# A fused two-layer MLP in bf16: another way in for the first block's input, and another order for its second product

## The chip, the cores and the metric

One core of one Trainium2 chip runs the whole program. The metric is the device time of one execution in microseconds, as a median over runs.

## The reference

```python
x  = randn(8, 1024, 1024)      # float32
w1 = randn(1024, 4096)
w2 = randn(4096, 1024)
h = x @ w1
h = 0.5 * h * (1 + tanh(sqrt(2 / pi) * (h + 0.044715 * h ** 3)))
return (h @ w2).astype(float32)
```

There are 8192 tokens. Each goes through 1024 to 4096 columns, GELU, and 4096 to 1024 columns. In 128x512 matmuls (a 128x128 block of weights against 512 columns) that is 4096 for the first product and 4096 for the second.

## The kernel before

Tokens are taken in 16 blocks of 512. Both weights are cast to bf16 by the load and stay in SBUF, the on-chip memory. A block's x has to be turned so that the hidden dimension lies on the partitions. The kernel writes a bf16 copy of it to DRAM (`phase0`), and reads that back through the transposing DMA (`xbar`). The head of the program queues block 0's x, then w1, then block 1's x copies, then w2:

```python
def load_w1(j):                      # eight loads, 1 MB each as stored
    nc.gpsimd.dma_start(out=w1_sb[:, :, j*512:(j+1)*512], in_=w1r[:, :, j*512:(j+1)*512])
def load_w2(j):                      # eight loads of four 128-row chunks
    nc.gpsimd.dma_start(out=w2_sb[:, j*4:(j+1)*4, :], in_=w2r[:, j*4:(j+1)*4, :])
# ... cut
for hc in range(HC):
    phase0(0, hcs=[hc])              # strided copy of x into DRAM, as bf16
    xbar(0, hcs=[hc])                # transposing DMA into xT
# ... cut
for j in range(NW1):
    load_w1(j)
if NB > 1:
    phase0(1)
for j in range(NW2):
    load_w2(j)
for b in range(NB):
    # ... cut: xbar(b + 1), phase0(b + 2)
    g = mm1_gelu(b)                  # 32 chunks of 8 matmuls, GELU per two chunks
    mm2_store(b, g)
```

The second product goes slice after slice: 128 tokens run through all 32 chunks of w2 before the next 128 tokens begin.

```python
def mm2_store(b, g):
    for s in range(TSUB):                          # four slices of 128 tokens
        po = psum_o.tile([P, OC, NFREE], F32)
        for ic in range(IC):                       # 32 chunks of w2
            for oc in range(OC):
                nc.tensor.matmul(po[:, oc, :], lhsT=g[:, ic, s*P:(s+1)*P],
                                 rhs=w2_sb[:, ic, oc*NFREE:(oc+1)*NFREE],
                                 start=(ic == 0), stop=(ic == IC - 1))
        o_sb = opool.tile([P, OC, NFREE], F32)
        nc.vector.tensor_copy(out=o_sb, in_=po)
        # ... cut: store o_sb
```

## Time and profile before

| | before |
|---|---|
| time, median of 13 runs | 1821.73 us (1819.48 to 1823.04) |
| TensorE busy, of the profiled span | 1768.4 of 1820.8 us |
| first block-0 matmul | 20.2 us |
| block 1's first matmul | 158.2 us |
| last matmul, about | 1816 us |

(The prediction was made on the first four of these runs, with a median of 1822.65 us.)

The first part of the profile's page gives busy time by engine. PE is TensorE's matmuls, PEld its weight loads, which run beside them; DVE is VectorE, ACT is ScalarE, POOL is GpSimd; x is the number of instructions recorded:

```profile
PE 1768.4 (97%) x8029; PEld 803.1 (44%) x8192; DVE 78.4 (4%) x64; ACT 263.2 (14%) x257; POOL 92.0 (5%) x148
```

No other engine is busy for more than 15% of the span. The steady rate comes from a stretch table: from 300 to 400 us it counts 464 weight loads, one for each matmul, so about 0.2155 us each. The 256 matmuls of block 1's first product (158.20 to 213.45 us) give 0.2158 us, the figure used below. 8192 of them take about 1768 us. Some 50 us are not matmuls at full rate, and TensorE's timeline for the first 220 us shows where they are. Its columns are start, duration, engine, line, operation, tiles, count, and in brackets the idle time before and what ended it:

```profile
20.17 1.89 PE L117 MATMUL ph<-xT,w_sb 128*128 128x512 bf16 x4 [20.17 <-DMA w_sb<-in_w_dram]
24.51 0.58 PE L117 MATMUL ph<-xT,w_sb 128*128 128x512 bf16 x1 [2.46 <-DMA xT<-xb]
27.97 0.59 PE L117 MATMUL ph<-xT,w_sb 128*128 128x512 bf16 x1 [2.87 <-DMA xT<-xb]
31.47 0.58 PE L117 MATMUL ph<-xT,w_sb 128*128 128x512 bf16 x1 [2.92 <-DMA xT<-xb]
34.90 56.20 PE L117 MATMUL ph<-xT,w_sb 128*128 128x512 bf16 x244 [2.84 <-DMA xT<-xb]
90.93 8.80 PE L137 MATMUL po<-w_sb,g 128*128 128x512 bf16 x40
101.37 1.89 PE L137 MATMUL po<-w_sb,g 128*128 128x512 bf16 x7 [1.64 <-DMA w_sb<-in_w_dram]
106.99 2.78 PE L137 MATMUL po<-w_sb,g 128*128 128x512 bf16 x8 [3.74 <-DMA w_sb<-in_w_dram]
112.10 46.26 PE L137 MATMUL po<-w_sb,g 128*128 128x512 bf16 x196 [2.33 <-DMA w_sb<-in_w_dram]
158.20 55.42 PE L117 MATMUL ph<-xT,w_sb 128*128 128x512 bf16 x251
```

The waits of the same engine, summed by what they waited for:

```profile
PE ph L117 <- DMA w_sb<-in_w_dram: 20.2, 1, 20.2
PE ph L117 <- DMA xT<-xb: 11.1, 4, 2.9
PE po L137 <- DMA w_sb<-in_w_dram: 7.7, 3, 3.7
```

Read them together. TensorE does nothing for 20.2 us. It then gets x one piece at a time until 34.9 us, when only seven matmuls are done. The first product then runs without a break, if slowly at first. Slice 0 of the second product starts at 90.9 us and catches up with the w2 loads, which it waits for three times, until 112.1 us. From 158.2 us on nothing is lost any more.

The third loss is a matter of rate. In this stretch table (columns: stretch, length, then for each engine busy time and number of instructions, granted TensorE clock, share of the DMA engines, GB/s) only 10 and 16 matmuls are recorded in two 4 us stretches that elsewhere hold 19 to 21:

```profile
112.00:116.00 4.00, 3.90 (x10) 1.43 (x10) 0.29 (x1) 0.00 (x0) 3.10 (x6) 0.50 1.81 178
116.00:120.00 4.00, 4.00 (x16) 1.57 (x14) 0.93 (x1) 0.00 (x0) 2.47 (x5) 0.74 1.98 171
120.00:124.00 4.00, 3.95 (x19) 1.86 (x19) 0.00 (x0) 0.00 (x0) 1.80 (x3) 1.00 1.81 167
```

The granted clock (the share of TensorE's full clock that the profile records) is 0.50 and 0.74 there: after the waits the matmuls start again at half speed. They do so at 34.9 us as well, where the weight loads stand 0.43 us apart until 39.55 us. (The clock column says 1.00 in that first stretch, so the spacing is the safer sign.)

### The profile page before, as it was taken

How to read it: one execution, taken by the hardware profiler on the slowest of the kernel's cores; microseconds unless marked ns; L12 is line 12 of the kernel's file. 1: busy time of each engine (PE TensorE's matmuls, PEld its weight loads, DVE VectorE, ACT ScalarE, POOL GpSimd, SP SyncE). 2: the span in 40 equal slices, each digit the busy share in tenths (PEclk: the TensorE clock that was granted, in tenths of full speed). 3: DMA queues.
4: the chain of work that ended last, by engine and by line, in shares of the span. 5: the costliest groups of instructions: out<-in, count | busy, mean ns of one | idle time of the engine just before them, and what ended most of it. 6: DMA issues, size and time to landing. Idle time of an engine off the chain costs nothing.

```text
span 1820.8 us, 17187 instructions
## 1 busy us (share of the span) xinstructions
PE 1768.4 (97%) x8029; PEld 803.1 (44%) x8192; DVE 78.4 (4%) x64; ACT 263.2 (14%) x257; POOL 92.0 (5%) x148
## 2 busy tenths in 40 slices
PE   3989999999999999999999999999999999999998
PEld 1434444444444444444444444444444444444444
DVE  0000010000000000000000000000000000000000
ACT  0201202011030210202012020110202102020120
POOL 3237300000000000000000000000000000000000
PEclk9989999999999999999999999999999999999999
DMA  9999910101001010010101101010010100100001
GB/s 174 198 195 194 117 47 1 47 24 35 35 1 58 12 35 35 15 44 12 47 24 23 47 1 46 24 35 35 1 58 12 35 35 15 44 12 24 24 0 47
DMA packets 159047, 85.02 MB, mean 47 GB/s; under 512 B 138496, under 2 KB 146688, under 8 KB 158976
## 3 DMA queue, kind: packets, MB, share of 16 engines
q0 software_dynamic: 80128, 33.56, 14.8%
q1 hardware_dynamic: 78848, 50.35, 9.4%
q8 instruction: 64, 1.05, 0.3%
q14 instruction: 7, 0.06, 0.0%
HBM read 67.11 MB, written 50.33 MB: 65 GB/s over the span
## 4 chain that ended last, share of the span: by engine, by line
PE 93%; DMA 5%; issue 1%; POOL 1%; DVE 0%; POOLq 0%
PE po L137 48%; PE ph L117 45%; DMA w_sb<-in_w_dram 5%; DMA xb<-in_x_dram 0%; POOL w_sb L73 0%; POOL xb L92 0%; DVE o_sb L145 0%; POOLq L185 0%
## 5 line engine op out<-in xcount | busy, mean ns | idle before, releaser
L117 PE MATMUL ph<-xT,w_sb 128*128 128x512 bf16 x4016 | 886.9, 380 | 35.5 <-DMA w_sb<-in_w_dram 20.2
L137 PE MATMUL po<-w_sb,g 128*128 128x512 bf16 x4013 | 886.4, 380 | 12.0 <-DMA w_sb<-in_w_dram 7.7
L117 PEld LDWEIGHTS <-w_sb 128*128 128x128 bf16 x4096 | 401.4, 98 | 518.0 <-DMA w_sb<-in_w_dram 20.2
L137 PEld LDWEIGHTS <-g 128*128 128x128 bf16 x4096 | 401.7, 98 | 494.4 <-issue 13.4
L124 ACT ACTIVATE g<-ph 128x1024 bf16<-128x1024 f32 x256 | 261.9, 1023 | 1497.9 <-PE ph L117 1478.4
L145 DVE COPY o_sb<-po 128x1024 f32<-128x1024 f32 x64 | 78.4, 1224 | 1738.9 <-PE po L137 1701.1
L92 POOL DMA_DIRECT2D xb<-in_x_dram x128 | 78.8, 617 | 109.3 <-DMA w_sb<-in_w_dram 82.2
L64 POOL DMA_DIRECT2D w_sb<-in_w_dram x8 | 7.0, 898 | 1.3 <-DMA xb<-in_x_dram 1.3
L73 POOL DMA_DIRECT2D w_sb<-in_w_dram x8 | 6.0, 781 | 0.2 <-issue 0.2
L124 ACT ACT_TABLE_LOAD x1 | 1.3, 1283 | 0.7 <-PEq L185 0.7
L185 POOL MEMSET const-float32-0.0<- 128x1 f32 x1 | 0.1, 98 | 0.2 <-issue 0.2
L185 POOL MEMSET const-bfloat16-1.0<- 128x1 bf16 x1 | 0.1, 101 | 0.0
L185 POOL MEMSET const-float32-1.0<- 128x1 f32 x1 | 0.1, 98 | 0.0
L185 POOL MEMSET const-uint8-127<- 128x1 uint8 x1 | 0.1, 98 | 0.0
## 6 DMA issues: line engine op xcount, KB each, us to landing
out_dram<-o_sb SPq DMA_DIRECT2D x64, 512.0 KB, 3.8
xb<-in_x_dram POOLq DMA_DIRECT2D x128, 128.0 KB, 5.6
w_sb<-in_w_dram POOLq DMA_DIRECT2D x16, 1024.0 KB, 30.5
xT<-xb SPq DMA_TRANSPOSE x128, 2.6
```

The source lines that it names most:

```text
L64: nc.gpsimd.dma_start(out=w1_sb[:, :, j * W1_COL:(j + 1) * W1_COL], in_=w1r[:, :, j * W1_COL:(j + 1) * W1_COL],)
L73: nc.gpsimd.dma_start(out=w2_sb[:, j * W2_ROWG:(j + 1) * W2_ROWG, :], in_=w2r[:, j * W2_ROWG:(j + 1) * W2_ROWG, :],)
L92: nc.gpsimd.dma_start(out=xb[hc], in_=xr[hc])
L117: nc.tensor.matmul(ph[:, k, :], lhsT=w1_sb[:, hc, ic * P:(ic + 1) * P], rhs=xT[:, hc, :], start=(hc == 0), stop=(hc == HC - 1),)
L124: nc.scalar.activation(out=g[:, ig * IPB:(ig + 1) * IPB, :], in_=ph, func=GELU,)
L137: nc.tensor.matmul(po[:, oc, :], lhsT=g[:, ic, s * P:(s + 1) * P], rhs=w2_sb[:, ic, oc * NFREE:(oc + 1) * NFREE], start=(ic == 0), stop=(i ...
L145: nc.vector.tensor_copy(out=o_sb, in_=po)
L185: nc = _bacc.Bacc("TRN2", target_bir_lowering=False, num_devices=1)
```

## The change

It wants to start TensorE earlier and to stop it from waiting for w2. It has four parts:

- **x of block 0** comes by four plain loads into SBUF, is transposed by TensorE against an identity, and is copied by VectorE from PSUM, the memory that the matmuls' results go to here.
- **w1** comes in smaller pieces: the first 512 columns in eight (one for each hidden chunk), the others in four each. **w2** comes in 32 pieces.
- **Block 0's second product** goes through w2 chunk by chunk, with all four slices accumulating at once.
- **PSUM**: that needs four accumulators, so the two pools of two buffers become one pool of four.

```diff
-    psum_h = ... bufs=2          psum_o = ... bufs=2
+    pspool = ... bufs=4
-    def load_w1(j):
-        nc.gpsimd.dma_start(out=w1_sb[:, :, c0:c1], in_=w1r[:, :, c0:c1])
+    def load_w1(j, split):
+        for h0 in range(0, HC, HC // split):
+            h1 = h0 + HC // split
+            nc.gpsimd.dma_start(out=w1_sb[:, h0:h1, c0:c1], in_=w1r[:, h0:h1, c0:c1])
 # ... cut: load_w2 by single chunks
+        if ic_major:
+            pos = [pspool.tile([P, OC, NFREE], F32, name="ps") for _ in range(TSUB)]
+            for ic in range(IC):
+                for s in range(TSUB):
+                    for oc in range(OC):
+                        nc.tensor.matmul(pos[s][:, oc, :], lhsT=g[:, ic, s*P:(s+1)*P], ...)
+            # ... cut: then four copies and four stores
-    for hc in range(HC):
-        phase0(0, hcs=[hc])
-        xbar(0, hcs=[hc])
+    for s in range(TSUB):
+        nc.gpsimd.dma_start(out=x0_sb[:, s, :], in_=x2[s*P:(s+1)*P, :])
+    make_identity(nc, ident)
+    for s in range(TSUB):
+        pt = pspool.tile([P, 2, HC, P], BF16, name="ps")
+        for hc in range(HC):
+            nc.tensor.transpose(pt[:, 0, hc, :], x0_sb[:, s, hc*P:(hc+1)*P], ident)
+        nc.vector.tensor_copy(out=xT0[:, :, s*P:(s+1)*P], in_=pt[:, 0])
+    load_w1(0, split=HC)
+    for j in range(1, NW1):
+        load_w1(j, split=4)
 # ... cut
-        mm2_store(b, g)
+        mm2_store(b, g, ic_major=(b == 0))
```

## The prediction

> **What bounds the kernel now.** TensorE. The profile's first part has PE busy 1768.4 of 1820.8 us. The stretch table shows 464 weight loads, one per matmul, in 100 us, so a 128x512 matmul costs 0.2158 us; 8192 need about 1767 us. Only time below full rate can be won. In order of time, TensorE's rows show it before 158.2 us, where block 1 begins:
>
> - 0 to 34.9 us: 20.2 us for the first w1 megabyte, which stood behind the strided x copies, then 11.1 us in four waits for x chunks through the transposing DMA. Seven matmuls were done.
> - About 2.4 us lost to half-speed matmuls (12 at 0.43 us) from 34.9 us.
> - 7.7 us in three waits of block 0's second product for w2 (wait table). It walks all 32 w2 chunks in 13.8 us, but a w2 megabyte lands only each 5.6 us, the last at 112.1 us.
> - About 3 us at half speed after these stalls (granted clock 0.50 at 108 to 116 us).
>
> **What the change does.**
>
> 1. Block 0's x: four plain loads (2 MB fp32 read), 32 transposes on TensorE, four PSUM copies by VectorE, in place of 8 DRAM copies and 8 DMA transposes. Undisturbed w1 loads land 1 MB (2 MB read) each 5.05 us (208 GB/s at 36 to 56 us); data first moves at about 2.7 us. Estimate from these: x in SBUF at 8 to 8.5 us, its last copy (about 1.2 us, as the old 1024-element copy) done at 10.5 to 11 us.
> 2. First w1 megabyte in eight pieces right behind x: the last lands at about 13.5 us. First accumulation ends at about 13.9 us instead of 35.3: 21 us won. Later w1 megabytes land each 5.05 us against 6.9 us of matmuls for each, so no wait.
> 3. The half-speed start remains, 2 to 3 us. The Trainium skill, "TensorE: Matmul & The Clock Gate", Part 1, states a warm-up of about 3.4 us (this trace: 4.7 us).
> 4. Block 0's second product goes chunk by chunk over four accumulators: 1.73 us of matmuls per w2 chunk, 55 us in all. It starts at about 70 us; w2 flows from about 55 us, a chunk (1/4 MB) each 1.4 us, done by about 100. All w2 waits (7.7 us) and the second cold stretch (3 us) go.
> 5. Added: changing the four PSUM buffers between phases of block 0: about 0.1 us in, 0.3 us out. 80 smaller load issues on GpSimd, about 0.4 us each, hide under the transfers.
>
> Sum: block 1 starts at 13.9 + 53.5 + 2.5 + 0.1 + 55.2 + 0.3 = 125.5 us instead of 158.2. All of it is on the critical path: 32.7 us.
>
> **Predicted: 1790 us, 80% range 1785.5 to 1796; faster by over 2% (below 1786.2) 0.12, within 2% 0.86, slower 0.02.**
>
> **What would show it right.** First accumulation complete at 13 to 15 us; no PE wait for w2; one half-speed stretch only; block 1's first matmul at 123 to 129 us; then the same 0.2158 us per matmul.
>
> **What would make it wrong.** The identity's construction on GpSimd delaying w1's issue; eight DMAs in flight (GpSimd's issues wait for the one eight back) being too few for the smaller transfers, so w1 slips below 208 GB/s; slower warm-up; block 1's x transposes arriving after 125 us; or faster x loading, which would pass 2%.

## The result

| | before | after |
|---|---|---|
| time, median | 1821.73 us (13 runs) | 1789.10 us (8 runs, 1788.72 to 1789.85) |
| TensorE busy, of the profiled span | 1768.4 of 1820.8 us | 1766.3 of 1787.7 us |
| first block-0 matmul (not a transpose) | 20.2 us | 12.0 us |
| second product of block 0 starts | 90.9 us | 69.6 us |
| block 1's first matmul | 158.2 us | 125.1 us |

The ratio of the times is 0.9822, with a 95% interval of 0.9812 to 0.9832. Here and below a ratio is the mean time of one kernel's runs over that of the other's of the same rounds, so it is not quite the ratio of the medians quoted. At a limit of 2% this counts as the same. The interval lies clear of 1, so the 1.8% is real.

The page's busy times, the timeline and the waits of TensorE, after:

```profile
PE 1766.3 (99%) x8060; PEld 804.8 (45%) x8224; DVE 80.9 (5%) x68; ACT 263.2 (15%) x257; POOL 117.5 (7%) x198
```

```profile
4.92 1.03 PE L170 MATMUL ps<-ident,x_sb 128*128 128x128 bf16 x8 [4.92 <-DMA x_sb<-in_x_dram]
6.25 1.03 PE L170 MATMUL ps<-ident,x_sb 128*128 128x128 bf16 x8 [0.30 <-DMA x_sb<-in_x_dram]
8.87 1.03 PE L170 MATMUL ps<-ident,x_sb 128*128 128x128 bf16 x8 [1.59 <-DMA x_sb<-in_x_dram]
10.14 1.03 PE L170 MATMUL ps<-ident,x_sb 128*128 128x128 bf16 x8 [0.24 <-DMA x_sb<-in_x_dram]
11.96 57.84 PE L107 MATMUL ps<-xT,w_sb 128*128 128x512 bf16 x251 [0.78 <-DVE xT L171]
69.64 55.42 PE L128 MATMUL ps<-w_sb,g 128*128 128x512 bf16 x251
125.08 55.41 PE L107 MATMUL ps<-xT,w_sb 128*128 128x512 bf16 x251
180.33 55.42 PE L147 MATMUL ps<-w_sb,g 128*128 128x512 bf16 x250
```

```profile
PE ps L170 <- DMA x_sb<-in_x_dram: 7.0, 4, 4.9
PE ps L107 <- DVE xT L171: 0.8, 1, 0.8
```

The four rows of L170 are the transposes, eight in 1.03 us, each set after its x piece has landed. From 11.96 us on three rows follow each other without idle time: the first product, the second product chunk by chunk (L128), block 1. No wait for w2 is left. Block 1 starts 33.1 us earlier and then takes what it took before (180.33 - 125.08 = 55.25 us for 256 matmuls, 0.2158 us each), so all of the gain lies before it: from block 1's start to the end of the span it is 1662.6 us in both profiles.

TensorE's weight loads show how the first product got going. The load of a matmul's weights starts when its piece of w1 is there:

```profile
12.77 0.15 PEld L107 LDWEIGHTS <-w_sb 128*128 128x128 bf16 x1 [0.28 <-DMA w_sb<-in_w_dram]
13.40 0.10 PEld L107 LDWEIGHTS <-w_sb 128*128 128x128 bf16 x1 [0.48 <-DMA w_sb<-in_w_dram]
...
15.35 0.13 PEld L107 LDWEIGHTS <-w_sb 128*128 128x128 bf16 x2 [0.57 <-DMA w_sb<-in_w_dram]
15.75 0.15 PEld L107 LDWEIGHTS <-w_sb 128*128 128x128 bf16 x1 [0.27 <-issue]
16.18 0.15 PEld L107 LDWEIGHTS <-w_sb 128*128 128x128 bf16 x1 [0.28 <-issue]
16.55 2.47 PEld L107 LDWEIGHTS <-w_sb 128*128 128x128 bf16 x12 [0.22 <-issue]
```

From 12.77 to 15.35 us the pieces of w1 set the pace. They come about 0.64 us apart, more slowly than even a half-speed matmul (0.43 us). At 16.55 us the full rate is reached. From the last piece on, three matmuls took 1.20 us in place of 0.65, so the half-speed start costs only some 0.55 us. About 0.4 us of that comes after the first accumulation (eight matmuls), which is through at about 15.8 us.

### The profile page after: what moved, and what is told of

It reads as the page before. It is cut to its first block, busy times and chain, and to the rows that moved or that the text cites. A ratio compares the mean times of both kernels' runs of the same rounds, so it can differ in the third digit from the quotient of the medians.

```text
span 1787.7 us, 17292 instructions
## 1 busy us (share of the span) xinstructions
PE 1766.3 (99%) x8060; PEld 804.8 (45%) x8224; DVE 80.9 (5%) x68; ACT 263.2 (15%) x257; POOL 117.5 (7%) x198
## 4 chain that ended last, share of the span: by engine, by line
PE 94%; DMA 5%; issue 1%; POOL 0%; DVE 0%; POOLq 0%
PE ps L107 46%; PE ps L147 46%; DMA w_sb<-in_w_dram 4%; PE ps L128 2%; DMA x_sb<-in_x_dram 0%; DMA xb<-in_x_dram 0%; POOL x_sb L164 0%; POOL w_sb L67 0%; DVE o_sb L155 0%; POOL w_sb L73 0%; POOLq L203 0%
## 5 line engine op out<-in xcount | busy, mean ns | idle before, releaser
L107 PE MATMUL ps<-xT,w_sb 128*128 128x512 bf16 x4016 | 884.8, 380 | 5.2 <-DVE xT L171 0.8
L147 PE MATMUL ps<-w_sb,g 128*128 128x512 bf16 x3761 | 826.8, 379 | 4.1
L114 ACT ACTIVATE g<-ps 128x1024 bf16<-128x1024 f32 x256 | 261.9, 1023 | 1464.7 <-PE ps L107 1445.3
L155 DVE COPY o_sb<-ps 128x1024 f32<-128x1024 f32 x60 | 73.5, 1224 | 1582.2 <-PE ps L147 1531.9
L88 POOL DMA_DIRECT2D xb<-in_x_dram x120 | 73.7, 616 | 44.1 <-DMA xb<-in_x_dram 24.2
L128 PE MATMUL ps<-w_sb,g 128*128 128x512 bf16 x251 | 55.2, 379 | 0.3
L128 PEld LDWEIGHTS <-g 128*128 128x128 bf16 x256 | 25.0, 98 | 30.2
L67 POOL DMA_DIRECT2D w_sb<-in_w_dram x36 | 24.0, 680 | 14.4 <-DMA w_sb<-in_w_dram 11.6
L73 POOL DMA_DIRECT2D w_sb<-in_w_dram x32 | 16.9, 529 | 27.6 <-DMA w_sb<-in_w_dram 23.1
L170 PE MATMUL ps<-ident,x_sb 128*128 128x128 bf16 x32 | 4.1, 309 | 7.0 <-DMA x_sb<-in_x_dram 7.0
L137 DVE COPY o_sb<-ps 128x1024 f32<-128x1024 f32 x4 | 4.6, 1217 | 111.9 <-PE ps L128 111.9
L170 PEld LDWEIGHTS <-x_sb 128*128 128x128 bf16 x32 | 3.1, 140 | 7.8 <-DMA x_sb<-in_x_dram 7.8
```

The costliest lines, as they stand in the source:

```text
L67: nc.gpsimd.dma_start(out=w1_sb[:, h0:h1, c0:c1], in_=w1r[:, h0:h1, c0:c1],)
L73: nc.gpsimd.dma_start(out=w2_sb[:, ic, :], in_=w2r[:, ic, :],)
L88: nc.gpsimd.dma_start(out=xb[hc], in_=xr[hc])
L107: nc.tensor.matmul(ph[:, k, :], lhsT=w1_sb[:, hc, ic * P:(ic + 1) * P], rhs=xT[:, hc, :], start=(hc == 0), stop=(hc == HC - 1),)
L114: nc.scalar.activation(out=g[:, ig * IPB:(ig + 1) * IPB, :], in_=ph, func=GELU,)
L128: nc.tensor.matmul(pos[s][:, oc, :], lhsT=g[:, ic, s * P:(s + 1) * P], rhs=w2_sb[:, ic, oc * NFREE:(oc + 1) * NFREE], start=(ic == 0), sto ...
```

## The experiments

Two questions are put. Does the gain divide into a share of the head and a share of the new order, as the prediction's list suggests? And what sets the start in the first 16 us?

Theory A for the first question: with slice-after-slice order, block 1 can't start before three slices of matmuls have followed the last w2 chunk. The head alone would then be mostly spent waiting. Rival B: the listed gains add. The kernels of the first question ran on one chip (before: 1821.68 us), but for the one with w2 ahead. A gain in us is against the median of the kernel before in the same rounds, unless the text says otherwise.

**Head alone.**

```diff
-        mm2_store(b, g, ic_major=(b == 0))
+        mm2_store(b, g, ic_major=False)
```

> The changed kernel with block 0's second product back in its old order (one 128-token slice after the other); the new head is kept. Theory A (the gains do not add: with the slice-after-slice order block 1 starts 41.4 us of matmuls and a 3 us cold stretch after the last w2 chunk lands, so the earlier start is mostly spent waiting for w2): the last chunk lands at about 107 us, block 1 starts at 151 to 153 us, time 1814 to 1818 us; PE waits for w2 total 20 us or more. Rival B (the gains add as the prediction listed them, 21 us for the head and 10.7 us for the order): 1800 us.

Measured: 1815.24 us, ratio 0.9963 (0.9948 to 0.9978). TensorE's waits and a part of its timeline:

```profile
PE ps L147 <- DMA w_sb<-in_w_dram: 11.8, 22, 1.7
```

```profile
69.46 3.62 PE L147 MATMUL ps<-w_sb,g 128*128 128x512 bf16 x15
...
91.25 1.01 PE L147 MATMUL ps<-w_sb,g 128*128 128x512 bf16 x2 [0.47 <-DMA w_sb<-in_w_dram]
92.69 1.01 PE L147 MATMUL ps<-w_sb,g 128*128 128x512 bf16 x2 [0.43 <-DMA w_sb<-in_w_dram]
...
106.85 43.99 PE L147 MATMUL ps<-w_sb,g 128*128 128x512 bf16 x191 [1.69 <-DMA w_sb<-in_w_dram]
150.67 55.42 PE L107 MATMUL ps<-xT,w_sb 128*128 128x512 bf16 x251
```

The second product starts at 69.5 us, 21 us earlier than in the kernel before. It then goes two matmuls at a time as chunks land, about 1.45 us apart, and from 76.8 us on at half speed. The last chunk comes at 106.85 us against 112.1 us before. Block 1 starts at 150.7 us, only 7.5 us earlier than before. The time was as A had it, and block 1's start 0.3 us earlier than A's 151 to 153 us. The expected sum of the waits (20 us or more) missed as written: the row shows 11.8 us, because the half-speed pairs fill part of the time between chunks and count as busy.

**Order alone.** The kernel before with only `ic_major=(b == 0)` and the shared pool of four PSUM buffers.

```diff
-        mm2_store(b, g)
+        mm2_store(b, g, ic_major=(b == 0))
```

> The kernel before with only the chunk-by-chunk order (and the four shared PSUM buffers). Theory A: first accumulation still ends at about 35 us, no PE wait for w2, no second half-speed stretch, block 1 at 146 to 147 us, time 1810 to 1812 us, so a gain of 10 to 12 us. A and B agree here; together with the head alone, A has the two parts sum to 17 us of 32.6, B to all of it.

Measured: 1810.34 us, ratio 0.9937 (0.9920 to 0.9954).

```profile
35.48 55.35 PE L116 MATMUL ps<-xT,w_sb 128*128 128x512 bf16 x244 [2.84 <-DMA xT<-xb]
90.66 55.42 PE L137 MATMUL ps<-w_sb,g 128*128 128x512 bf16 x251
146.10 55.41 PE L116 MATMUL ps<-xT,w_sb 128*128 128x512 bf16 x251
```

The unbroken stretch begins at 35.48 us (at half speed until 38.4 us), there is no wait for w2, and block 1 starts at 146.10 us. The head alone gained 6.4 us and the order alone 11.3 us, 17.8 us together (from unrounded medians). Both at once gain 32.6 us (in the rounds of the result). Some 15 us belong to neither part: the head's time becomes a gain only when the second product no longer waits for the end of w2. B is refuted.

**Head alone, w2 ahead of block 1's x.** If the last w2 chunk sets block 1's start, moving that chunk must move the time, with matmuls, bytes and order of products untouched.

```diff
+    for ic in range(IC):
+        load_w2(ic)
     if NB > 1:
         phase0(1)
-    for ic in range(IC):
-        load_w2(ic)
```

> The head alone (old order of block 0's second product), with w2's loads queued before block 1's x copies. Theory A (block 1's start follows the last w2 chunk): the last chunk lands at 90 to 95 us in place of 107, block 1 starts at 134 to 140 us, time 1798 to 1804 us, 12 to 16 us below the head alone, though the matmuls and bytes are the same. Rival: w2's landing isn't what holds it, same time as the head alone within 3 us.

Measured: 1799.59 us, ratio 0.9886 (0.9869 to 0.9902). That is a gain of 20.8 us, where the head alone had 6.4 us.

```profile
91.63 42.47 PE L147 MATMUL ps<-w_sb,g 128*128 128x512 bf16 x191 [0.70 <-DMA w_sb<-in_w_dram]
133.93 55.42 PE L107 MATMUL ps<-xT,w_sb 128*128 128x512 bf16 x251
```

The last chunk came 15.2 us earlier than in the head alone and block 1 16.7 us earlier. From last chunk to block 1 it is 42.3 us here and 43.8 us in the head alone. The chunk's own two matmuls and three slices are 41.9 us (194 times 0.2158), and the rest is the half-speed restart (until 92.4 us here, until 111.0 us in the head alone). So the last chunk sets block 1's start, and this is shown. Block 1's start came 0.07 us before A's range.

**Coarse loads.**

```diff
-    load_w1(0, split=HC)
+    load_w1(0, split=1)
-        load_w1(j, split=4)
+        load_w1(j, split=1)
 # w2: eight loads of four chunks
```

> The changed kernel with w1 in eight loads and w2 in eight loads, as before. Theory A: bytes and their order in the queue are the same, w1's first megabyte lands whole at 15 to 16 us; the first accumulation is no longer done while it lands and its half-speed stretch is exposed, block 1 starts 2 to 4 us later, time 1791 to 1793 us; w2's grain costs nothing. Rival: the fine loads are what made the start early, 1797 us or more; or they are idle, 1789 us.

Measured: 1792.19 us (1790.94 to 1793.23), ratio 0.9837 (0.9823 to 0.9852). The first megabyte of w1 landed whole at 15.29 us, the same time as the last of the eight pieces (15.35 us), and the half-speed matmuls came after it. Block 1 started at 127.37 us. So the fine w1 loads are worth 2 to 3 us (2.3 us by block 1's start, 3.1 us by the time), by hiding the half-speed start under the landing. No wait for w2 appears with four-chunk loads.

**Old x path.**

```diff
-    # four loads, identity, 32 transposes, four copies
+    for hc in range(HC):
+        phase0(0, hcs=[hc])
+        xbar(0, hcs=[hc])
```

> The changed kernel with block 0's x by the old way (eight strided copies in DRAM, eight DMA transposes), fine loads and the chunk-by-chunk order kept. Theory A: the x path is what delays the start, the first accumulation ends at 33 to 36 us, time 1809 to 1812 us, as with the order alone. Rival (fine w1 loads win a good part of the head's gain by themselves): 1797 to 1804 us.

Measured: 1809.53 us (1808.84 to 1811.55), ratio 0.9935 (0.9920 to 0.9949). That is the order alone, within 1 us. TensorE's first w1 wait ended at 14.6 us here, earlier than the 20.2 us of before, but x came through the transposing DMA until 34.0 us all the same. The x path made the start late; the w1 pieces alone win nothing that the runs resolve.

The head with w2 ahead ran on a second chip, together with the next three (before: 1820.38 us). For the second question: the prediction counted a wait until 13.9 us and then 2.5 us lost to half speed, as two terms. Theory A: they cover each other, so taking one away leaves the other. The effects are small, and the changed kernel was not in these rounds. The gains below are therefore against its 1789.10 us from other rounds; against the kernel before of the same rounds, the ratios of the three kernels (0.9825, 0.9825, 0.9820) do not differ from the 0.9822 of the change. So block 1's start in the profile is given beside the times. In the changed kernel it is 125.08 us, and 124.70 us in a second profile of it (told below): differences under some 0.4 us are not resolved.

**Early matmuls on zeros.** 20 matmuls whose result nobody reads, 8 before the transposes and 2, 5, 2 and 3 after each group of them.

```diff
+    wz = wpool.tile([P, NFREE], BF16)
+    nc.vector.memset(wz, 0.0)
+    def warm(n):
+        pw = pspool.tile([P, OC, NFREE], F32, name="ps")
+        for _ in range(n):
+            nc.tensor.matmul(pw[:, 0, :], lhsT=wz[:, :P], rhs=wz, start=True, stop=True)
```

> The changed kernel with 20 matmuls on a zero tile that nobody reads, before and between the transposes, so that the clock is up when the first real matmul comes. Theory A (the half-speed start is hidden, because w1's pieces land each 0.64 us against 0.43 us for a half-speed matmul until 15.4 us): gain 0.3 to 1.0 us, 1788 to 1789 us. Rival (the prediction's term: 2 to 3 us are lost to the half-speed start): 1786 to 1787 us.

Measured: 1788.74 us, ratio 0.9825 (0.9810 to 0.9840), block 1 at 124.41 us. The first matmul came at 11.41 us at full speed, but the eighth could not start before 15.22 us, when its piece of w1 landed (15.35 us in the changed kernel). By the time that is a gain of 0.4 us, by block 1's start of 0.7 us (0.3 us against the second profile). That is small, as A had it, and not the rival's 2 to 3 us.

**First w1 columns in four loads of 128.**

```diff
-    load_w1(0, split=HC)
+    for c in range(W1_COL // P):
+        nc.gpsimd.dma_start(out=w1_sb[:, :, c*P:(c+1)*P], in_=w1r[:, :, c*P:(c+1)*P])
```

> The changed kernel with the first 512 columns of w1 cut into four loads of 128 columns (all of one output chunk's weights) in place of eight loads of one row block. The first accumulation then needs a quarter of the bytes. Theory A: it no longer waits for w1, starts at 12 us and runs at half speed until 15.5 to 16.5 us, which costs what the wait cost: gain 0 to 1.5 us, 1787.5 to 1789 us. Rival (the wait for w1 bytes alone sets the start): gain of 3 us or more.

Measured: 1789.14 us, ratio 0.9825 (0.9811 to 0.9840), block 1 at 124.88 us. No wait for w1 after the start at 11.46 us, but weight loads 0.43 us apart until 16.97 us. The time shows no gain (it is 0.14 us above A's range), and the 0.2 us by block 1's start are below what two profiles resolve. So no gain is shown, which is the lower end of A's 0 to 1.5 us; the rival's 3 us or more is excluded.

**Both.** The two edits above together.

> Both together. Theory A (wait for w1 and half speed cover the same 4 us, so that only taking away both pays): first matmul at about 11 to 12 us at full speed, gain 2.5 to 4 us, 1785 to 1786.6 us. Rival (the two are separate terms, each worth its own): the sum of the gains of the two runs alone.

Measured: 1787.87 us, ratio 0.9820 (0.9805 to 0.9834), block 1 at 123.67 us. The gain of 1.2 us by the time (1.4 us by block 1's start) is more than the rival's sum (0.4 us and nothing; 0.9 us by block 1's starts) and less than A's 2.5 to 4 us. Against the second profile of the changed kernel the comparison is 1.0 us with a sum of 0.1 us. Within these rounds, every run of this kernel is below every run of the other two: the column loads win 0.9 us on top of the early matmuls and nothing alone. A's number missed. The timeline shows what took the rest:

```profile
11.74 7.94 PE L107 MATMUL ps<-xT,w_sb 128*128 128x512 bf16 x36 [0.22 <-DMA w_sb<-in_w_dram]
19.89 0.61 PE L107 MATMUL ps<-xT,w_sb 128*128 128x512 bf16 x2 [0.21 <-DMA w_sb<-in_w_dram]
21.17 47.23 PE L107 MATMUL ps<-xT,w_sb 128*128 128x512 bf16 x213 [0.68 <-DMA w_sb<-in_w_dram]
```

TensorE had finished the first 512 columns early and now waited for the next 512. Those still came cut by rows, so that no chunk could be finished before all four pieces had landed.

**The first 2048 columns in loads of 128, with the early matmuls.** This ran on a third chip, as did the single x load below (before: 1820.20 us).

```diff
-    load_w1(0, split=HC)
-    for j in range(1, NW1):
+    for c in range(4 * W1_COL // P):
+        nc.gpsimd.dma_start(out=w1_sb[:, :, c*P:(c+1)*P], in_=w1r[:, :, c*P:(c+1)*P])
+    for j in range(4, NW1):
```

> Early matmuls on zeros and the first 2048 columns of w1 (four megabytes as stored) in loads of 128 columns. In the run of both together, TensorE had finished the first 512 columns at about 18.6 us and then waited for the second 512, cut by rows, until 21.2 us. Theory A' (the start then runs into w1's stream: what a product chunk needs must land chunk by chunk, about 1.4 us each against 1.73 us of matmuls): no wait for w1 after the first, block 1 starts at 122.0 to 122.8 us, time 1786.2 to 1787.2 us. Rival (the remaining 1.3 us or so was something else, such as the smaller pieces): no change from 1787.9 us, or slower.

Measured: 1786.65 us (1785.97 to 1786.98), ratio 0.9816 (0.9803 to 0.9830).

```profile
11.94 55.43 PE L107 MATMUL ps<-xT,w_sb 128*128 128x512 bf16 x251 [0.21 <-DMA w_sb<-in_w_dram]
67.20 55.42 PE L128 MATMUL ps<-w_sb,g 128*128 128x512 bf16 x251
122.64 55.41 PE L107 MATMUL ps<-xT,w_sb 128*128 128x512 bf16 x251
```

All 256 matmuls of the first product now take 55.3 us (67.20 - 11.94), which is the full rate, and block 1 starts at 122.64 us. Theory A' (the start now runs into w1's stream, and column loads there free it) holds.

Since the changed kernel had been timed on another chip, both were run once more, with no further edit, in the same rounds (before: 1822.01 us).

> The changed kernel unaltered, on the same chip and in the same rounds as the next run, because the early-matmul version was timed on another chip than the changed kernel: 1787.5 to 1789.5 us.

Measured: 1789.27 us (1788.18 to 1789.92), ratio 0.9822 (0.9808 to 0.9835). Its profile is the second one of the changed kernel: block 1 starts at 124.70 us.

> The version with early matmuls and column loads again. If its lead is real: 2.0 to 3.0 us below the changed kernel of the same rounds, every run below every run of that. If it was the chip: within 1 us.

Measured: 1786.64 us (1786.02 to 1786.89), ratio 0.9807 (0.9794 to 0.9821). Every run of it is below every run of the changed kernel, by 2.6 us at the medians; block 1 starts at 122.52 us against 124.70 us. This version beats both kernels, if only by 0.15% over the change. Against the kernel before its interval holds the 2% limit, so by that limit it is unclear. The column loads of 2048 columns were not run without the early matmuls.

**Block 0's x in one load.** The prediction had the last of x on the chip at 8 to 8.5 us, and it came at 10.14 us.

```diff
-    for s in range(TSUB):
-        nc.gpsimd.dma_start(out=x0_sb[:, s, :], in_=x2[s*P:(s+1)*P, :])
+    nc.gpsimd.dma_start(out=x0_sb, in_=x2[0:TB, :].rearrange("(s p) h -> p s h", p=P))
```

> The changed kernel with block 0's x in one load of 1 MB (as stored) in place of four. The four landed at 4.9, 6.2, 8.9 and 10.1 us where the prediction had 8 to 8.5 us for the last; the transfers dip from about 5 to 7 us. If the many small issues cause the dip: the load lands at 8 to 9 us and the dip is gone. If not (the kernel before has a dip at the same time): it lands at 9.5 to 10.5 us. All transposes then come after it, so the whole is 1 to 3 us slower than the changed kernel.

Measured: 1788.97 us, one run of unknown state. The transposes began at 9.78 us. Two stretches of the changed kernel, the second of them once more from its second profile, then the same two of this one:

```profile
3.00:4.00 1.00, 0.00 (x0) 0.00 (x0) 0.00 (x0) 0.00 (x0) 1.00 (x3) 1.00 0.95 168
...
5.00:6.00 1.00, 0.95 (x8) 0.68 (x8) 0.01 (x1) 0.00 (x0) 1.00 (x3) 1.00 0.84 139
```

```profile
5.00:6.00 1.00, 0.87 (x8) 0.77 (x8) 0.00 (x0) 0.00 (x0) 1.00 (x3) 1.00 1.02 178
```

```profile
3.00:4.00 1.00, 0.00 (x0) 0.00 (x0) 0.00 (x0) 0.00 (x0) 1.00 (x3) 1.00 0.81 98
...
5.00:6.00 1.00, 0.00 (x0) 0.00 (x0) 0.00 (x0) 0.00 (x0) 1.00 (x3) 1.00 1.15 211
```

The dip is not there (211 GB/s in place of 139), but the start is slower (98 GB/s in place of 168, and 172 in the second profile). x lands 0.4 us earlier than in the first profile and 0.1 us earlier than in the second (9.84 us). As the unaltered kernel's own dip was half gone in its second profile (178 GB/s), this run does not show that the four loads cause it. What makes either loss stays open. My forecast of a slower whole missed too, and the reason is a find:

```profile
9.78 3.31 PE L169 MATMUL ps<-ident,x_sb 128*128 128x128 bf16 x32 [9.78 <-DMA x_sb<-in_x_dram]
13.90 55.41 PE L107 MATMUL ps<-xT,w_sb 128*128 128x512 bf16 x251 [0.81 <-DVE xT L170]
69.15 55.42 PE L128 MATMUL ps<-w_sb,g 128*128 128x512 bf16 x251
```

The 32 transposes ran back to back for 3.3 us, and the first product then took 55.25 us for 256 matmuls (69.15 - 13.90): full speed from its first matmul. Its weight loads show the same, 29 of them recorded in 6.14 us from 13.90 us. The trace even shows when the clock rose: the transposes start 0.107 us apart until 12.64 us and 0.056 us apart from 12.71 us, so the full clock came 2.9 us after they began, with no other work on TensorE before it. In both profiles of the changed kernel, where the same transposes come in four bursts of 1.03 us, the matmuls after them start at half speed.

## Why the prediction was right

The time was 1789.1 us for 1790, well inside the range, and block 1 started at 125.08 us for 125.5. Point by point:

| term of the prediction | predicted | measured |
|---|---|---|
| last x piece landed | 8 to 8.5 us | 10.14 us |
| first accumulation done | 13.9 us | about 15.8 us |
| lost to half speed after it | 2.5 us | about 0.4 us |
| second product starts | about 70 us | 69.64 us |
| all of w2 landed | about 100 us | about 107 us |
| wait for w2 | none | none |
| one half-speed stretch only | yes | yes |
| PSUM hand-over at block 0's end | 0.3 us | 0.2 us (125.08 - 69.64 - 256 times 0.2158) |
| block 1 starts | 125.5 us | 125.08 us |
| matmul after that | 0.2158 us | 0.2158 us |

The mechanism held: the gain is all TensorE time before block 1, it lies wholly on the critical path, and no later block changed. Within the sum, two terms were off by about 2 us each, in opposite directions, and the second error follows in part from the first. That they cancel to 0.4 us is in part luck: the prediction added a wait and a half-speed loss that in the runs overlap, and it had the wait too short by about as much.

- **Step 1, "x in SBUF at 8 to 8.5 us"**, was too early. It took the steady rate from the first byte. The single-load run shows 98 GB/s from 3 to 4 us and 9.78 us until the transposes could begin. The four-load kernel dips to 139 GB/s between 5 and 6 us (178 in its second profile, where the last x came at 9.84 us). x and the first w1 pieces were late by about 2 us. The VectorE copies were cheaper than estimated: 0.69 us each in place of about 1.2 us. That saved little, as only the last copy is waited for.
- **Step 3, "the half-speed start remains, 2 to 3 us"**, was too large for this kernel. Most of the half-speed stretch passed under the wait for w1's pieces. The early-matmul run (0.4 us of the time) and the column-load run (nothing, with 13 half-speed matmuls) show that either limit alone holds the start.
- **Step 4, "done by about 100"** for w2, was 7 us early. The chunks came 1.45 us apart, close to the 1.4 us estimated, but the first landed only at about 62 us. Step 5's 0.4 us for a load issue on GpSimd was too low as well: it took 0.53 to 0.77 us. Neither mattered: the last chunk is needed at about 123 us (69.64 + 31 times 1.73) and is there at 107.

The list could mislead in one thing. It books "21 us won" by the head and 10.7 us by the order (7.7 and 3). As the sum of both, made at once, that is right to 1 us (31.7 for 32.6). As two separate values it is wrong: the head alone gained 6.4 us.

On the Trainium skill: "TensorE: Matmul & The Clock Gate", Part 1, has about 3.4 us of sustained work before the full clock. The traces agree roughly, with a wide spread: 2.9 us of transposes in the single-load run and 2.9 us of matmuls in the coarse-load and order-alone runs, 4.7 us in the kernel before, 4.6 us from the first matmul in the changed one (11.96 to 16.55 us, with the array partly waiting), 5.5 us in the column-load run (11.46 to 16.97 us).

## What to carry to other kernels

When TensorE is full in the steady state, look for the gain in the program's first block, and ask of every part of the head which transfer its consumer will wait for next: an earlier start is worth only as much as the slowest stream behind it allows. A loop order that uses each arriving weight chunk for all the work it can serve turns a wait for a stream into overlap. Two limits that cover the same microseconds, here the half-speed clock and the landing of w1, must be taken away together, and the next one in the stream is then close behind. In this kernel that was worth 1.2 us, and 2.6 us once the next was gone too.

## What the Trainium skill lacked or had wrong

- "TensorE: Matmul & The Clock Gate", Part 4, says of PE transposes that full speed ("HAM K=8/8") "doesn't engage" for them. The runs differ in two ways. Transposes run faster once the clock is up: eight took 0.62 us after early matmuls, 1.03 us without. And they count towards the clock: of 32 back to back (3.31 us) the last started 0.056 us apart in place of 0.107, and the matmuls after them ran at the full rate from the first one (256 in 55.25 us); one run shows this. In four bursts of 1.03 us with gaps they did not suffice.
- The same section gives about 390 ns for a transpose alone and 275 ns in one kernel, and no figure for transposes back to back. As a duration the trace agrees (309 ns mean in the changed kernel), but back to back they cost far less: 32 in 3.31 us, 0.107 us each at half speed.
- "DMA: Bandwidth & Descriptors", section "Anatomy of one DMA", fits a load from GpSimd as 2.0 us and the bytes at 436 GB/s. For the 2 MB float32 load that is cast to 1 MB, an estimate from that page gives 6.8 us. The run shows 8.5 us from issue to landing, as the first load of the program with w1's loads behind it. The page has nothing on a slow first stretch (98 GB/s as stored from 3 to 4 us, against about 200 later); one run shows this figure.
